# Hybrid conformer and neighbourhood-attention layer: the first two output tiles' preparation, moved behind other work on three queues

## The chip, the cores and the metric

The kernel runs on one core of a Trainium2 chip, in one launch. The metric is the time on the device in microseconds (us). The kernel before took 1469.12 us, the median of 3 runs (1467.73 to 1469.58). TensorE (PE in the rows) multiplies matrices, VectorE (DVE), ScalarE (ACT) and GpSimd (POOL) work on elements, and SyncE (SP) issues all transfers. Each engine runs its own instructions strictly in its queue's order; engines wait for each other by semaphores.

## The reference

One encoder layer over two batches that share all weights: 512 and 1024 tokens, each with 16 meta tokens in front, 1024 channels, float32. In short:

```python
u = rms_norm(h, pre_g)
z = einsum('bld,de->ble', u, w_in)       # 1024 -> 7 x 1024
c_val, c_glu, c_gate, q, k, v, a_gate = split(z)
conv = silu(layer_norm(depthwise_conv31(c_val * sigmoid(c_glu)) + conv_b)) * silu(c_gate)
att  = neighbourhood_attention(q, k, v, meta keys, rel_bias) * silu(a_gate)   # 16 heads of 64
y    = einsum('ble,ed->bld', concat(conv, att), w_out)                        # 2048 -> 1024
out  = h + rms_norm(y, post_g)                                                # meta rows dropped
```

The attention looks at a window of 8 rows by 16 columns of a token grid 64 wide, plus the 16 meta keys, with a relative bias, and takes a softmax over both. The layer norm of the convolution runs over the 1024 channels of a token.

## The kernel before

The 1536 grid tokens are held as three grids of 512 tokens. To keep float32 accuracy each product is three passes of a two-part format (`proj`, L175 to L181: high weights by high input, low weights by high input, high weights by low input). One gate, which is one 128-channel column of one grid, is 24 matmuls of 128x512. ScalarE makes the high part of a weight (L141), GpSimd the low part (L142).

The work goes through these stages:

- The pre-norm, and the input projections.
- The depthwise convolution of 31 taps on VectorE (L272). Its result z goes to memory (`zs`) by channel; the conv gates go to `cgd`.
- The attention in 8 pairs of heads, each with 3 grids and 2 halves (`groups`). For every block of queries: scores on TensorE (L578), reading them with the bias and taking the maximum on VectorE (L585), its negative (L588), the exponential on ScalarE (L589), reciprocal and scaling on VectorE (L590, L591), transposes on TensorE (L600), their copy on ScalarE (L602, `pT`), the weighted product with the values (L616, `po`). At the end of a grid VectorE copies `po` to `mo` (L620), and SP stores it to `mad` (L621). Other projections and gates are put between these steps to fill TensorE.
- The layer norm's statistics are woven into the last pairs (`statistics`, L648 on). Mean and variance of each token go to `std` in memory; at the end the variances come back as `rv`, become 1/sqrt (L678, L679), and are stored again (`std<-rv`, L680), 6 KB in pieces of 4 bytes.
- After the attention, the last six attention gates (`a_gate(6, 7)`): 6 times 24 matmuls, a copy to `ag` on ScalarE (L342), a store to `agd` (L343).
- The output product in 12 tiles of 128 tokens (L794). `load_wo(n)` loads the n-th of 16 row blocks of w_out (L738) into `wraw`, `xr` or `yo`, and makes its high part on ScalarE (L748) and its low part on VectorE (L749).

`mix(t, parts)` (L757 to L774) prepares tile t. Part 0 is the conv half: it loads mean and 1/sqrt (`mb`, L755), z (`mx<-zs`, L764) and the conv gate (`gt<-cgd`, L765), subtracts and multiplies on VectorE (L767, L768), takes 8 silus of 128x128 and one silu of the gate on ScalarE (L770, L771), multiplies them (L772), and makes the high part `mh` on ScalarE (L773) and the low part `ml` on VectorE (L774). Part 1 is the attention half: the same from L771 on, with `mad` and `agd`. TensorE takes the first two tiles together: first half of tile 0, first half of tile 1, second half of tile 0, second half of tile 1, each of 48 matmuls.

What sets the order: the functions are traced in the order in which they are written, and a scheduler with its own model of times then puts each engine's instructions into that engine's queue. `tc.issue_after(ins)` is a tie for it: what is traced under it on the engine of `ins` is queued behind `ins`. It adds no semaphore wait. Tiles 0 and 1 are prepared under such ties: `mix(0, (0,))` behind the last `pT` copy on ScalarE, and `mix(1, (0,))` behind the copy of the last gate, both on ScalarE alone.

Of the kernel before, what the change touches and what calls it, by code (L numbers as in the profile page):

```python
# [13 lines left out]
ALU = mybir.AluOpType  # L14
# [79 lines left out]
def tile_encoder(ctx: ExitStack, tc: tile.TileContext, mt, xn, w_main, w_v, wo, cw, cb, lg, lb, pg, postg, rbt, rmask, y):  # L94
    nc = tc.nc
# [3 lines left out]
    mad = [tc.dram_tile((DC, 128, 512), F32, name=f"mad{g}") for g in range(3)]  # L99
# [46 lines left out]
    def new_mm():  # L146

        pool, tag = banks[1][banks[0] % len(banks[1])]
        banks[0] += 1
        return pool.tile([128, 512], F32, name=tag, tag=tag)  # L150
# [14 lines left out]
    def use_w(ec):  # L165

        w = ahead.pop(ec) if ec in ahead else load_w(ec)
        i = wseq.index(ec) + 1
        if i < len(wseq) and wseq[i] not in ahead:
            ahead[wseq[i]] = load_w(wseq[i])  # L170
        return w
# [3 lines left out]
    def proj(ps, hi, lo, c0, c1):  # L175
        n = c1 - c0
        uh, ul = u_cols(c0, c1)
        for dc in range(DC):
            for i, (w, u) in enumerate(((hi, uh), (lo, uh), (hi, ul))):
                last_mm[0] = nc.tensor.matmul(ps[:, :n], lhsT=w[:, dc, :], rhs=u[dc // 4][:, dc % 4, :],  # L180
                                              start=(dc == 0 and i == 0), stop=(dc == DC - 1 and i == 2)).ins  # L181
# [99 lines left out]
        nc.scalar.copy(out=zc.rearrange("p (b r c) -> p b r c", r=8, c=8), in_=z[:, i].rearrange("p (r b c) -> p b r c", r=8, b=8))  # L281
        nc.sync.dma_start(zs[i][c], zc)

    vws, metas, last_copy = {}, [], [None]

    def load_v(qv):
        raws, his, los = [], [], []
# [46 lines left out]
    def gates(base, dst, cs):  # L334

        ws = [use_w(base + c) for c in cs]
        for g in range(3):
            for c, (wh, wl) in zip(cs, ws):
                ps = new_mm()
                proj(ps, wh, wl, 16 + g * 512, 16 + g * 512 + 512)  # L340
                gt = gpool.tile([128, 512], F32, name="ag", tag="ag", bufs=2)
                last_copy[0] = nc.scalar.copy(out=gt, in_=ps).ins  # L342
                nc.sync.dma_start(dst[g][c], gt)  # L343
                yield

    def c_gate(*cs):
        return gates(16, cgd, cs)

    def a_gate(*ps):
        return gates(40, agd, ps)  # L350
# [192 lines left out]
    def block(g, j):  # L543

        e = ebufs[g][{0: 1, 7: 2}.get(j, 0)]
        if g == 0:
            return min(max(j - 1, 0), 5), 3, "k3", 2, 108, e
        R8 = GR[g]["R"] * 8
        if j in (0, 7):
            return min(j, 6), 2, "k2", 2, R8, e  # L550
        return j - 1, 3, "k3", 3, R8, e

    def load_values(p, g):
        esl = slice(p * 128, p * 128 + 128)
        R8 = GR[g]["R"] * 8
        if g == 0:
            vt = apool.tile([108, 2, 6, 128], F32, name="vp", bufs=VPB)
            for ch, p0, b0, k0, n in ((0, 0, 0, 0, 72), (0, 72, 1, 0, 36), (1, 0, 1, 36, 36), (1, 36, 2, 0, 72)):
                nc.sync.dma_start(vt[p0:p0 + n, ch], vd[b0:b0 + 6, k0:k0 + n, esl].rearrange("b k e -> k b e"))
        else:  # L560
            vt = apool.tile([104, 8, 128], F32, name="vt", bufs=2)
            nc.sync.dma_start(vt[:R8], vd[:, GR[g]["vrow"] * 8:GR[g]["vrow"] * 8 + R8, esl].rearrange("b k e -> k b e"))
        vts[p, g] = vt

    def scores(p, g, hf):
        if hf == 0:
            load_values(p, g)
        kh, kl = kbufs[p]
        qh, ql = qbuf.pop((p, g, hf))
        R8 = GR[g]["R"] * 8  # L570
        for jj in range(4):
            j = hf * 4 + jj
            b0, nk, key, _, _, e = block(g, j)
            ra, rn, ro = GR[g][key]
            w = rn * 8
            ss = ps_s.tile([128, 512], F32, name="ss")
            for i, (q, k) in enumerate(((qh, kh), (qh, kl), (ql, kh))):
                last_qk[0] = nc.tensor.matmul(ss[:, :nk * w], lhsT=q[:, jj].rearrange("p h x -> p (h x)"),  # L578
                                 rhs=k[:, b0:b0 + nk, ra:ra + rn, :].rearrange("p b r c -> p b (r c)"),
                                 start=(i == 0), stop=(i == 2))  # L580
            sv_ = ss[:, :nk * w].rearrange("p (k x) -> p k x", k=nk)[:, :, ro * 8:ro * 8 + R8]
            pt = apool.tile([128, 312], F32, name="pt", bufs=PTB)
            pv = pt[:, :nk * R8]
            sm = apool.tile([128, 4], F32, name="sm", bufs=8)
            nc.vector.tensor_tensor_reduce(out=pv.rearrange("p (k x) -> p k x", k=nk), in0=sv_,  # L585
                                           in1=e.rearrange("p k r c -> p k (r c)"), scale=1.0,
                                           scalar=-3.0e38, op0=ALU.add, op1=ALU.max, accum_out=sm[:, 0:1])
            nc.vector.tensor_scalar(out=sm[:, 1:2], in0=sm[:, 0:1], scalar1=-1.0, scalar2=None, op0=ALU.mult)  # L588
            last[0] = nc.scalar.activation(out=pv, in_=pv, func=AF.Exp, bias=sm[:, 1:2], scale=1.0, accum_out=sm[:, 2:3])  # L589
            nc.vector.reciprocal(sm[:, 3:4], sm[:, 2:3])  # L590
            nc.vector.tensor_scalar(out=pv, in0=pv, scalar1=sm[:, 3:4], scalar2=None, op0=ALU.mult)  # L591
            pts[p, g, j] = pv

    def transposes(p, g, hf):
# [10 lines left out]
    def weighted(p, g, hf):  # L605
        if hf == 0:
            pos[p, g] = ps_o.tile([128, 8, 64], F32, name="po")
        po, vt = pos[p, g], vts[p, g]
        for j in range(hf * 4, hf * 4 + 4):
            b0, _, _, nt, kt, _ = block(g, j)  # L610
            pT = pTs.pop((p, g, j))
            for k in range(nt):
                for h in range(2):
                    hs = slice(h * 64, h * 64 + 64)
                    v = vt[:, k, b0, hs] if g == 0 else vt[:kt, b0 + k, hs]
                    last_pv[0] = nc.tensor.matmul(po[hs, j, :], lhsT=v, rhs=pT[:kt, k * 128 + h * 64:k * 128 + h * 64 + 64],  # L616
                                                  start=(k == 0), stop=(k == nt - 1)).ins
        if hf == 1:
            mo = apool.tile([128, 512], F32, name="mo", bufs=1)
            nc.vector.tensor_copy(out=mo, in_=pos.pop((p, g)).rearrange("p j x -> p (j x)"))  # L620
            nc.sync.dma_start(mad[g][p], mo)  # L621

    def inner_gates():
        for p in (3, 4, 5):
# [56 lines left out]
        yield  # L681

    stats = statistics()
    knext, last_pv, last_pt = [None], [None], [None]
    e_build(0)
    groups = [(p, g, hf) for p in range(NPAIR) for g in range(3) for hf in range(2)]
    for n in range(len(groups) + 2):
        if n < len(groups):
            p, g, hf = groups[n]
# [62 lines left out]
    def moments(t):  # L752
        tsl = slice(t * 128, t * 128 + 128)
        s = std[:, tsl]
        nc.sync.dma_start(mb, bass.AP(s.tensor, s.offset, [[0, 128], [TG, 2], [1, 128]]))  # L755

    def mix(t, parts=(0, 1)):  # L757
        for part in parts:
            if part == 0:
                moments(t)  # L760
            mx, gt = mxs[part], gts[part]
            mh, ml = [x[t % 2 * 2 + part] for x in (mhs, mls)]
            g, csl = t // 4, slice(t % 4 * 128, t % 4 * 128 + 128)
            nc.sync.dma_start(mx, (zs, mad)[part][g][:, :, csl].rearrange("c p t -> p c t"))  # L764
            nc.sync.dma_start(gt, (cgd, agd)[part][g][:, :, csl].rearrange("c p t -> p c t"))  # L765
            if part == 0:
                nc.vector.tensor_tensor(out=mx, in0=mx, in1=mb[:, 0:1].broadcast_to([128, 8, 128]), op=ALU.subtract)  # L767
                nc.vector.tensor_tensor(out=mx, in0=mx, in1=mb[:, 1:2].broadcast_to([128, 8, 128]), op=ALU.mult)  # L768
                for c in range(8):
                    nc.scalar.activation(out=mx[:, c], in_=mx[:, c], func=AF.Silu, scale=lg_sb[:, c:c + 1], bias=lb_sb[:, c:c + 1])  # L770
            nc.scalar.activation(out=gt, in_=gt, func=AF.Silu)  # L771
            nc.vector.tensor_tensor(out=mx, in0=mx, in1=gt, op=ALU.mult)  # L772
            nc.scalar.copy(out=mh, in_=mx)  # L773
            (nc.vector if t < MLT else nc.gpsimd).tensor_tensor(out=ml, in0=mx, in1=mh.bitcast(F32), op=ALU.subtract)  # L774

    with tc.issue_after(last_pt[0]):
        mix(0, (0,))
    for n in range(16):
        if n == 6:
            mix(0, (1,))  # L780
        elif n == 8:
            with tc.issue_after(last_copy[0]):
                mix(1, (0,))
        elif n == 10:
            mix(1, (1,))
        load_wo(n)
    pgb = wop.tile([128, D], F32, name="pgb")
# [28 lines left out]
    for t in range(TG // 128):  # L816
# [26 lines left out]
        for hf in range(2):  # L843
            hsl = slice(hf * 512, hf * 512 + 512)
            nc.vector.scalar_tensor_tensor(out=yo[:, hsl], in0=yo[:, hsl], scalar=s4[:, 3:4], in1=xr[:, hsl],
                                           op0=ALU.mult, op1=ALU.add)
# [65 lines left out]
```

## Time and profile before

| | |
|---|---|
| median of 3 runs | 1469.12 us (1467.73 to 1469.58) |
| the profiled execution | 1470.34 us |
| its span in the trace | 1468.2 us |
| TensorE busy with matmuls | 1437.6 us, 98% of the span |
| VectorE busy | 1012.4 us, 69% |
| ScalarE busy | 562.8 us, 38% |
| GpSimd busy | 254.9 us, 17% |
| TensorE's share of the chain that ended last | 90% |

The profile is of one execution. Busy time tells which engine is full; the view of waits tells what an engine's idle time ended with; the timeline gives single instructions with the idle time in front of them in brackets; the windows give the granted clock of TensorE in a stretch, where 1.00 is 2.4 GHz and 0.50 is 1.2 GHz. The chain of waits is followed back from the last instruction.

### The profile page before, as it was taken

To read this page: it belongs to the slowest core of one execution; us is meant where nothing else is said; L and a number is where in the kernel's file an instruction comes from. 1 tells how busy PE (TensorE), PEld (TensorE's weight loads), DVE (VectorE), ACT (ScalarE), POOL (GpSimd) and SP (SyncE) were. 2 spreads that over 40 slices of the span, in tenths; PEclk is the share of its full clock that TensorE was granted. 3 is DMA by queue.
4 is the path that set the end of the run, shared out by engine and by line. 5 is a ranking of instruction groups with operands and counts; after the bars stand their busy time and mean duration, and the time that the engine had idled before them with its cause. 6 is when DMAs were issued, how large, how long until landed. Compare 5 with 4: busy or idle time off the path is not lost.

```text
span 1468.2 us, 24129 instructions
## 1 busy us (share of the span) xinstructions
PE 1437.6 (98%) x9536; PEld 1239.6 (84%) x9536; DVE 1012.4 (69%) x1739; ACT 562.8 (38%) x1299; POOL 254.9 (17%) x188
## 2 busy tenths in 40 slices
PE   7999999999999999999999999999979989999998
PEld 6988998988998888888888988888868878888886
DVE  6599999998999899846776777767544364342431
ACT  7311112112111111235564555655534466544440
POOL 2042022112101211221111211111101002122120
PEclk9999999999999999999999999999989999999999
DMA  8113113312231212242232232332322495544521
GB/s 266 42 48 117 47 55 110 93 40 93 76 92 50 96 51 86 105 105 75 77 88 79 84 82 77 88 87 83 86 62 87 159 294 145 151 147 136 164 89 43
DMA packets 153464, 145.19 MB, mean 99 GB/s; under 512 B 37216, under 2 KB 125432, under 8 KB 153352
## 3 DMA queue, kind: packets, MB, share of 16 engines
q1 hardware_dynamic: 153352, 143.67, 32.5%
q8 instruction: 74, 1.21, 0.3%
q14 instruction: 38, 0.31, 0.1%
HBM read 105.35 MB, written 42.72 MB: 101 GB/s over the span
## 4 chain that ended last, share of the span: by engine, by line
PE 90%; DMA 4%; ACT 2%; DVE 2%; POOL 1%; issue 1%; DVEq 0%; SPq 0%; ACTq 0%; POOLq 0%
PE mm L180 36%; PE py L794 18%; PE tp L180 9%; PE mm L322 5%; PE ss L578 5%; PE po L180 5%; PE po L616 4%; PE tp L600 4%; PE tp L322 3%; DMA wraw<-in_wo 1%; PE po L322 1%; POOL vl L142 1%; DMA std<-rv 1%; DMA yo<-in_wo 0%; ACT mx L770 0%
## 5 line engine op out<-in xcount | busy, mean ns | idle before, releaser
L180 PE MATMUL mm<-uw,whi 128*128 128x512 f32 (+2 forms) x1904 | 562.1, 372 | 0.0
L272 DVE SCALAR_TENSOR_TENSOR z<-ub,cw_sb,z 128x1536 f32<-128x1536 f32 (+2 forms) x270 | 498.7, 1854 | 8.1
L180 PEld LDWEIGHTS mm<-uw,whi 128*128 128x128 f32 x1904 | 342.5, 188 | 55.4 <-issue 1.3
L180 PE MATMUL mm<-uw,wlo 128*128 128x512 f32 (+2 forms) x952 | 352.6, 371 | 1.1 <-POOL wlo L142 1.1
L142 POOL TENSOR_TENSOR wlo<-wraw,whi 128x1024 fp32r<-128x1024 f32 x48 | 129.0, 2689 | 542.2 <-ACT whi L141 537.5
L180 PEld LDWEIGHTS mm<-uw,wlo 128*128 128x128 f32 x952 | 179.4, 188 | 27.2 <-POOL wlo L142 1.4
L794 PE MATMUL py<-uw,mh 128*128 128x512 f32 x576 | 182.0, 397 | 0.0
L180 PE MATMUL tp<-uw,whi 128*128 128x512 f32 (+2 forms) x512 | 132.9, 344 | 0.0
L589 ACT ACTIVATE pt<-pt,sm 128x216 f32<-128x216 f32 (+4 forms) x192 | 97.2, 507 | 92.9 <-DVE sm L588 79.9
L794 PEld LDWEIGHTS py<-uw,mh 128*128 128x128 f32 x576 | 108.7, 189 | 25.9
L794 PE MATMUL py<-uw,ml 128*128 128x512 f32 x288 | 113.8, 395 | 0.0
L602 ACT COPY pT<-tp 108x256 f32<-108x256 f32 (+4 forms) x192 | 77.9, 419 | 81.9 <-PE tp L600 57.1
L180 PEld LDWEIGHTS tp<-uw,whi 128*128 128x128 f32 x512 | 89.3, 188 | 11.6
L767 DVE TENSOR_TENSOR mx<-mx,mb 128x1024 f32<-128x1024 f32 x12 | 14.7, 1225 | 121.2 <-DMA mx<-zs 110.0
L585 DVE CUSTOM_DVE_ANT_0 pt<-ss,ei 128x216 f32<-128x216 f32 (+2 forms) x144 | 62.6, 437 | 50.2 <-PE ss L578 26.6
L180 PE MATMUL tp<-uw,wlo 128*128 128x512 f32 (+2 forms) x256 | 88.1, 344 | 0.0
L600 PE MATMUL tp<-ident,pt 128*96 128x128 f32 (+2 forms) x480 | 85.5, 275 | 0.3 <-ACT pT L602 0.2
L774 POOL TENSOR_TENSOR ml<-mx,mh 128x1024 fp32r<-128x1024 f32 x20 | 48.2, 2430 | 211.5 <-ACT mh L773 193.7
L322 PE MATMUL mm<-vh,uw 128*128 128x256 f32 x448 | 83.5, 285 | 0.7 <-DVE uw L208 0.5
L591 DVE TENSOR_SCALAR pt<-pt,sm 128x216 f32<-128x216 f32 (+4 forms) x192 | 70.7, 368 | 4.9
L578 PE MATMUL ss<-kh,qh 128*128 128x264 f32 (+3 forms) x192 | 65.3, 340 | 9.0 <-DVE sm L585 9.0
L141 ACT CAST whi<-wraw 128x1024 fp32r<-128x1024 f32 x48 | 50.2, 1047 | 61.6 <-DMA wraw<-in_w_main 19.1
(170 smaller groups left out, 2183.1 us busy)
## 6 DMA issues: line engine op xcount, KB each, us to landing
wraw<-in_w_main SPq DMA_DIRECT2D x48, 512.0 KB
xt<-in_xn SPq DMA_DIRECT2D x12, 512.0 KB
vd<-vs SPq DMA_DIRECT2D x96, 64.0 KB
zs<-zc SPq DMA_DIRECT2D x24, 256.0 KB
cgd<-ag SPq DMA_DIRECT2D x24, 256.0 KB
agd<-ag SPq DMA_DIRECT2D x24, 256.0 KB
ag<-zs SPq DMA_DIRECT2D x24, 256.0 KB
mad<-mo SPq DMA_DIRECT2D x24, 256.0 KB
```

Source lines behind the costliest of these rows:

```text
L142: eng.tensor_tensor(out=lo, in0=raw, in1=hi.bitcast(F32), op=ALU.subtract)
L180: last_mm[0] = nc.tensor.matmul(ps[:, :n], lhsT=w[:, dc, :], rhs=u[dc // 4][:, dc % 4, :], start=(dc == 0 and i == 0), stop=(dc == DC - 1 ...
L272: nc.vector.scalar_tensor_tensor(out=zv, in0=ub[:, a:b, k:k + 512], scalar=cw_sb[:, c, k:k + 1], in1=zv, op0=ALU.mult, op1=ALU.add)
L322: nc.tensor.matmul(ps[:, :256], lhsT=u[dc // 4][:, dc % 4, :], rhs=w[dc // 4][:, dc % 4, :], start=(dc == 0 and i == 0), stop=(dc == DC - ...
L578: last_qk[0] = nc.tensor.matmul(ss[:, :nk * w], lhsT=q[:, jj].rearrange("p h x -> p (h x)"), rhs=k[:, b0:b0 + nk, ra:ra + rn, :].rearrange ...
L585: nc.vector.tensor_tensor_reduce(out=pv.rearrange("p (k x) -> p k x", k=nk), in0=sv_, in1=e.rearrange("p k r c -> p k (r c)"), scale=1.0, ...
L589: last[0] = nc.scalar.activation(out=pv, in_=pv, func=AF.Exp, bias=sm[:, 1:2], scale=1.0, accum_out=sm[:, 2:3])
L591: nc.vector.tensor_scalar(out=pv, in0=pv, scalar1=sm[:, 3:4], scalar2=None, op0=ALU.mult)
L600: nc.tensor.transpose(out=tp[:kt, k * 128:k * 128 + 128], in_=pv[:, k * kt:k * kt + kt], identity=ident)
L602: last_pt[0] = nc.scalar.copy(out=pT[:kt, :nt * 128], in_=tp[:kt, :nt * 128]).ins
L616: last_pv[0] = nc.tensor.matmul(po[hs, j, :], lhsT=v, rhs=pT[:kt, k * 128 + h * 64:k * 128 + h * 64 + 64], start=(k == 0), stop=(k == nt - ...
L794: nc.tensor.matmul(pss[hf], lhsT=m[e // 8][:, e % 8], rhs=w[e][:, hf * 512:hf * 512 + 512], start=(n == 0 and i == 0), stop=(n == 15 and i ...
```

## The change

Three things are moved; no arithmetic is changed, and no instruction of the program's own is added or dropped.

- The first tile's conv half, `mix(0, (0,))`, gets two more ties: on VectorE behind the last scaling of the attention (L591), and on SP behind the next-to-last store of an attention result (L621).
- The second tile's conv half, `mix(1, (0,))`, is tied on ScalarE behind the copy of the fourth of the last six gates in place of the last, and is written at n = 6 of the loop over w_out in place of n = 8.
- The two attention halves are written later: `mix(0, (1,))` at n = 10 in place of 6, and `mix(1, (1,))` at n = 12 in place of 10.

```diff
-    vws, metas, last_copy = {}, [], [None]
+    vws, metas, copies = {}, [], []
...
-                last_copy[0] = nc.scalar.copy(out=gt, in_=ps).ins
+                copies.append(nc.scalar.copy(out=gt, in_=ps).ins)
...
-            nc.vector.tensor_scalar(out=pv, in0=pv, scalar1=sm[:, 3:4], scalar2=None, op0=ALU.mult)
+            last_norm[0] = nc.vector.tensor_scalar(out=pv, in0=pv, scalar1=sm[:, 3:4], scalar2=None, op0=ALU.mult).ins
...
-            nc.sync.dma_start(mad[g][p], mo)
+            stores.append(nc.sync.dma_start(mad[g][p], mo).ins)
...
-    knext, last_pv, last_pt = [None], [None], [None]
+    knext, last_pv, last_pt, last_norm, stores = [None], [None], [None], [None], []
...
-    with tc.issue_after(last_pt[0]):
+    with tc.issue_after(last_pt[0]), tc.issue_after(last_norm[0]), tc.issue_after(stores[-2]):
         mix(0, (0,))
     for n in range(16):
         if n == 6:
-            mix(0, (1,))
-        elif n == 8:
-            with tc.issue_after(last_copy[0]):
+            with tc.issue_after(copies[-3]):
                 mix(1, (0,))
         elif n == 10:
+            mix(0, (1,))
+        elif n == 12:
             mix(1, (1,))
         load_wo(n)
```

The first place is VectorE's queue in the last pair of heads. Here is what stood there before, in the first half of that pair; `mx` and `mb` are the first tile's.

```order
L585 ISA pt,sm<-ss,ei_5362 128x216
L585 ISA sm 128x1
L588 TENSOR_SCALAR sm<-sm 128x1
L590 RECIPROCAL sm<-sm 128x1
L767 TENSOR_TENSOR mx<-mx,mb 128x1024
L591 TENSOR_SCALAR pt<-pt,sm 128x216
L585 ISA pt,sm<-ss,ei_5362 128x216
```

The subtraction L767 stood between two steps of one block's softmax. Now the two steps of the first tile stand after the last block of the attention, between the last two copies of attention results:

```order
L590 RECIPROCAL sm<-sm 128x1
L591 TENSOR_SCALAR pt<-pt,sm 128x208
L620 COPY mo<-po 128x512
L767 TENSOR_TENSOR mx<-mx,mb 128x1024
L768 TENSOR_TENSOR mx<-mx,mb 128x1024
L620 COPY mo<-po 128x512
L772 TENSOR_TENSOR mx<-mx,gt 128x1024
```

The second place is ScalarE's queue during the last gates; `mh_12159` is the result of the second tile's conv half. Before, its 8 silus stood behind the copy of the sixth gate:

```order
L748 CAST uw<-xr 128x1024
L748 CAST uw<-yo 128x1024
L342 COPY ag<-mm 128x512
L770 ACTIVATE mx<-mx,lb_sb,lg_sb 128x128 x8
L771 ACTIVATE gt<-gt 128x1024
L748 CAST uw<-wraw 128x1024
L773 CAST mh_12160<-mx_12153 128x1024
L748 CAST uw<-wraw 128x1024
L773 CAST mh_12159<-mx 128x1024
```

Now they stand behind the fourth gate's copy, which is the first row here, and the fifth gate's copy comes after them:

```order
L342 COPY ag<-mm 128x512
L770 ACTIVATE mx<-mx,lb_sb,lg_sb 128x128 x2
L748 CAST uw<-wraw 128x1024
L770 ACTIVATE mx<-mx,lb_sb,lg_sb 128x128 x6
L771 ACTIVATE gt<-gt 128x1024
L748 CAST uw<-xr 128x1024
L748 CAST uw<-yo 128x1024
L773 CAST mh_12158<-mx_12153 128x1024
L748 CAST uw<-wraw 128x1024
L771 ACTIVATE gt_12154<-gt_12154 128x1024
L342 COPY ag<-mm 128x512
L748 CAST uw<-wraw 128x1024
```

The second tile's `mh_12159` is the row that follows these. The third place is the end of the attention on the same engine. Before, all copies of transposes were done when the gate's copy and the high part of the last gate's weights came:

```order
L602 COPY pT<-tp 104x384 x3
L602 COPY pT<-tp 104x256
L770 ACT_TABLE_LOAD
L770 ACTIVATE mx<-mx,lb_sb,lg_sb 128x128 x8
L771 ACTIVATE gt<-gt 128x1024
L342 COPY ag<-mm 128x512
L141 CAST whi<-wraw 128x1024
```

Now both stand in front of the last of these copies:

```order
L602 COPY pT<-tp 104x384 x4
L342 COPY ag<-mm 128x512
L141 CAST whi<-wraw 128x1024
L602 COPY pT<-tp 104x256
L770 ACT_TABLE_LOAD
L770 ACTIVATE mx<-mx,lb_sb,lg_sb 128x128 x8
```

The order of the attention's own steps in the last pair is also reshuffled by the scheduler, on TensorE, VectorE and ScalarE alike.

## Rows read from the trace of the kernel before

**Rows 1.** Page part 1: busy time, share of the span, instructions.

```profile
PE 1437.6 (98%) x9536; PEld 1239.6 (84%) x9536; DVE 1012.4 (69%) x1739; ACT 562.8 (38%) x1299; POOL 254.9 (17%) x188
```

**Rows 2.** Waits of TensorE: us in total, times, longest.

```profile
PE ss L578 <- DVE sm L585: 9.0, 2, 8.7
PE ss L202 <- DVE un L196: 8.4, 1, 8.4
PE py L794 <- ACT mh L773: 3.9, 1, 3.9
```

**Rows 3.** Timeline of TensorE: start, us, operation, count, idle time before and its end.

```profile
1079.24 0.59 PE L578 MATMUL ss<-kh,qh 128*128 128x264 f32 x1 [8.74 <-DVE sm L585]
...
1203.37 0.79 PE L794 MATMUL py<-woh,mh 128*128 128x512 f32 x1 [3.92 <-ACT mh L773]
```

**Rows 4.** Timeline of VectorE around the first wait.

```profile
1077.42 1.22 DVE L767 TENSOR_TENSOR mx<-mx,mb 128x1024 f32<-128x1024 f32 x1 [11.22 <-DMA mb<-std]
1078.56 0.33 DVE L591 TENSOR_SCALAR pt<-pt,sm 128x216 f32<-128x216 f32 x1
1078.81 0.38 DVE L585 CUSTOM_DVE_ANT_0 pt<-ss,ei 128x216 f32<-128x216 f32 x1
```

**Rows 5.** Chain that ended last: start, us, what.

```profile
1062.39 10.93 DMA std<-rv
1073.34 4.05 DMA mb<-std
...
1080.27 2.56 PE mm L180 x6
...
1083.37 2.53 PE mm L180 x11
...
1187.44 6.44 DMA yo<-in_wo
```

**Rows 6.** Windows: us, PE, PEld, DVE, ACT, POOL busy, PEclk, DMA share, GB/s.

```profile
112.00:114.00 2.00, 0.92 (x5) 0.53 (x3) 2.00 (x1) 1.31 (x3) 1.97 (x1) 1.00 0.41 96
...
1079.20:1083.10 3.90, 3.86 (x12) 3.15 (x13) 2.98 (x9) 2.02 (x6) 0.00 (x0) 0.50 0.13 34
...
1203.40:1209.40 6.00, 6.00 (x14) 4.74 (x15) 5.44 (x5) 3.72 (x4) 0.00 (x0) 0.50 1.02 274
1209.40:1215.00 5.60, 5.60 (x25) 4.49 (x25) 2.45 (x2) 2.28 (x6) 0.00 (x0) 1.00 0.51 159
```

**Rows 7.** Timeline of ScalarE, from the attention's end to the second tile.

```profile
1151.04 0.75 ACT L602 COPY pT<-tp 104x384 f32<-104x384 f32 x2 [4.19 <-PE tp L600]
...
1153.10 3.19 ACT L770 ACTIVATE mx<-mx,lb_sb,lg_sb 128x128 f32<-128x128 f32 x8
...
1157.61 1.05 ACT L141 CAST whi<-wraw 128x1024 fp32r<-128x1024 f32 x1
...
1194.92 0.58 ACT L342 COPY ag<-mm 128x512 f32<-128x512 f32 x1
1195.40 3.20 ACT L770 ACTIVATE mx<-mx,lb_sb,lg_sb 128x128 f32<-128x128 f32 x8
...
1202.27 1.05 ACT L773 CAST mh<-mx 128x1024 fp32r<-128x1024 f32 x1
```

**Rows 8.** Timeline of VectorE at the end of the attention.

```profile
1153.80 0.69 DVE L620 COPY mo<-po 128x512 f32<-128x512 f32 x1 [14.41 <-PE po L616]
```

**Rows 9.** Timeline of TensorE: last weighted product, and an earlier short wait.

```profile
114.03 0.39 PE L180 MATMUL mm<-uw,wlo 128*128 128x272 f32 x1 [1.11 <-POOL wlo L142]
...
1152.25 1.50 PE L616 MATMUL po<-pT,vt 104*64 104x64 f32 x44
```

**Rows 10.** Page part 5: costliest groups, count, busy us, mean ns, idle before.

```profile
L589 ACT ACTIVATE pt<-pt,sm 128x216 f32<-128x216 f32 (+4 forms) x192 | 97.2, 507 | 92.9 <-DVE sm L588 79.9
L585 DVE CUSTOM_DVE_ANT_0 pt<-ss,ei 128x216 f32<-128x216 f32 (+2 forms) x144 | 62.6, 437 | 50.2 <-PE ss L578 26.6
L591 DVE TENSOR_SCALAR pt<-pt,sm 128x216 f32<-128x216 f32 (+4 forms) x192 | 70.7, 368 | 4.9
```

## The prediction, made before the changed kernel had run

> **What bounds the kernel.** I read the busy times first. TensorE works in 98% of the span [rows 1], so a change of order can only win where TensorE stands still or runs slowly. The view of its waits comes next [rows 2]: three waits are over 3 us, one at the start of the kernel (8.4 us, on the pre-norm, which the change doesn't touch), one of 8.7 us on a VectorE step of the attention (L585), one of 3.9 us on ScalarE's `mh` (L773). The last two are in the stretches that the change touches. The timeline gives their places: TensorE stood for 8.74 us until 1079.24, and for 3.92 us until 1203.37 [rows 3].
>
> Who made the first one? VectorE's timeline shows L767, which belongs to the first output tile, in front of a scaling and a score reading of the attention [rows 4]. It stood for 11.22 us until `mb` had landed, and only behind it came L585, for which TensorE waited. The chain tells why `mb` was late: the store of the statistics began at 1062.39 and took 10.93 us, though the table of 1/sqrt is small, and the load behind it took 4.05 us [rows 5]. So a tile whose product starts only some 100 us later held up the attention.
>
> The second: the last gate's copy ran at 1194.92, the 8 silus behind it from 1195.40 to 1198.6, and `mh` from 1202.27 [rows 7]. The copy was itself late because the weight conversions in front of it in ScalarE's queue waited for a load that started at 1187.44 and took 6.44 us [rows 5]. TensorE had used up what it could do at 1203.37 − 3.92 = 1199.45.
>
> Both waits leave a second loss, seen in the windows: behind each the granted clock is 0.50, that is 1.2 GHz in place of 2.4 GHz, for 3.90 us after the first and 6.00 us after the second, and then 1.00 again [rows 6].
>
> **What the change removes.**
>
> 1. First wait: 8.74 us. Half clock behind it: 6 matmuls of L180 took 2.56 us there, 0.427 each, and 11 of them a little later 2.53 us, 0.230 each [rows 5]. So 3.90 us of that work would have taken 3.90 × 0.230/0.427 = 2.1, a loss of 1.8. Together 10.5.
> 2. Second wait: 3.92 us. Behind it 14 matmuls took 6.00 us [rows 6]; at 0.23 each, 3.2. Loss 2.8. Together 6.7.
>
> The sum of both is 17.2 us, if nothing takes their place.
>
> **What comes at the first tile's new place.** The two VectorE steps now stand between the last two copies L620. VectorE was idle there for 14.41 us until 1153.80, so from 1139.4 on [rows 8]. SP issues the tile's loads behind the store that follows the copy before that gap, so at about 1140. If `mb` takes 4.05 us and a 512 KB load 6.44 (the slowest such row I use) one behind the other [rows 5], the data are there at 1150.5, and two steps of 1.22 us [rows 4] end at 1152.9. The silus began at 1153.10 before [rows 7], behind the last transposes' copies, and are queued there still. So at the slowest in series the steps just end in time, and with the loads side by side some 4 us early; and this tile isn't wanted until the six gates are done, 144 × 0.230 = 33 us after the last weighted product. I cost it at nothing; the idle VectorE and the gates hide it. If that cover were gone the last copy L620 would wait, which holds nothing for TensorE but the attention half of the tiles, later still. SP has one thing less to wait for: the load of `mb` no longer stands in its queue behind the slow store of 10.93 us, so gate stores and weight loads queued behind it go out earlier, and I count nothing for this.
>
> **What comes at the second tile's new place.** I keep the old clock of the trace to see who is late. The last weighted product ended at 1152.25 + 1.50 = 1153.75 [rows 9]. With the cost of the next paragraph 1154.45. The fourth gate is done 96 × 0.230 = 22.1 us later, at 1176.5, and its copy (0.58 us, [rows 7]) at 1177.1. Behind it ScalarE does, up to the second tile's `mh`: 8 silus, 3.20 us; nine instructions of 1.05 us (conversions of weights, silus of gates, two `mh`), 9.45; and the fifth gate's copy, 0.58 [rows 7]. Together 13.2, so 1190.3. The weight loads in between could hold it: the queues carry loads of 6.44 us at worst [rows 5], and following the buffers with that landing for each load gives 1191.3. TensorE gets to the second tile after 144 + 48 matmuls: 1154.45 + 192 × 0.230 = 1198.6. The margin is 7 to 8 us, so the second wait goes wholly. What is late next are the attention halves, written 4 and 2 steps later now. They are wanted 48 and 96 matmuls later (11 and 22 us); ScalarE has for each only a silu, a conversion and its neighbours, so I find over 10 us of margin there. The fifth and sixth gates' copies now stand behind the silus: about 13 us at most, in a stage in which TensorE has other banks for its products and the output matmuls to go on with. Cost nothing.
>
> **What the change adds.** At the end of the attention the gate's copy and the conversion `whi` stand now in front of the last copy of transposes on ScalarE. The last weighted products wait for that copy, and TensorE with them. The trace of before has no such wait. At the one end, nothing: the gate's end and the weights may be early enough. At the other, copy and conversion run wholly in front, 0.58 + 1.05 = 1.63 us [rows 7]. A gain from it is excluded, since nothing on TensorE's path moves ahead. I take 0.7, below the middle, because ScalarE was idle 4.19 us just before that copy [rows 7] and part of the work falls into such a gap.
>
> The reshuffle of the attention's steps: the same instructions, with TensorE and VectorE in another order. Before, outside the stall, TensorE waited for L585 only 9.0 − 8.7 = 0.3 us in the whole kernel [rows 2]. I take nothing here as well; the bounds are in the rivals.
>
> **Sum.** 17.2 − 0.7 = 16.5 us of the profiled execution's 1470.34 us. That is 1.2 us above the median of the runs, so on the median: 1469.1 − 16.5 = 1452.6, which I round to 1452.5.
>
> **Rivals.**
>
> - *The second wait stays.* The silus move, but the `mh` behind them hangs on loads that hang on buffers that hang on VectorE's low parts; if one of those links is 8 us later than I followed it, ScalarE stands again, as it did for the load at 1187.44. For it: DMA share is 1.02 around 1203 to 1209 [rows 6], so loads are slow there. Against: the margin of 7 to 8 us already has 6.44 us for every load. Then only the first part is won: 1469.1 − 10.5 + 0.7 = 1459.3.
> - *The first wait only moves:* another step of the first tile or the store behind it gets in the attention's way, and only the second is won: 1469.1 − 6.7 + 0.7 = 1463.1. Against: the tie puts both steps behind the last L591, as the order shows, so this is the case in which the change doesn't do what it says.
> - *The new short wait costs the clock too.* What the rows show is a wait of 1.11 us at 114.03 [rows 9] in a window with the clock at 1.00 [rows 6], so a wait of that length left the clock whole; by that 0.7 us costs 0.7. Against me would be a half-clock stretch behind it as behind the two waits, 1.8 to 2.8 us: 1455. The Trainium skill, "TensorE: Matmul & The Clock Gate", section "A second HAM failure mode: psum-queue depth-cycling", speaks for this: it says that small idle gaps between groups of matmuls can be enough to make the clock fall and rise, with a cost each time. By that rule the time would be this rival's 1455; the trace, so far, agrees with the row at 114.03 instead.
> - *The reshuffled attention becomes a chain.* By the order of the queues 22 scores lie between the old place of the first wait and the end of the attention. If the new order makes TensorE wait, block by block, for reading, exponential and scaling of the block before, each costs up to 0.437 + 0.507 + 0.368 = 1.31 us [rows 10], 22 × 1.31 = 28.9 us, and the time is 1452.5 + 28.9 = 1481.4: slower than before. It decides from 16.5/22 = 0.75 us a block on; with reading and scaling alone (0.81) it would be 1470.2. For it: hundreds of places in TensorE's order differ. Against: VectorE had slack there, up to 14.41 us at a time near the end [rows 8], and the softmax of one block usually lies beside the projections that fill the gap.
>
> **Chances.** Forecast 0.72; second wait stays 0.09; clock lost too 0.06; first wait only moved 0.04; attention a chain 0.09. The last splits by its price per block: 0.01 still faster, 0.03 within 0.2%, 0.05 slower. 0.2% is 2.9 us, about what a measurement of this kernel can tell from no change. Faster: 0.72 + 0.09 + 0.06 + 0.04 + 0.01 = 0.92. Same 0.03, slower 0.05.
>
> The range: at the low end the added wait is nothing (1451.9) and some 2 us are left for the spread of the runs and for SP's earlier loads: 1450. At the high end the range takes in the full 1.63 us of the added wait (1453.5), the clock rival and the case in which the second wait stays (1459.3): 1459.5. That leaves out the moved wait and the chain, 0.13.
>
> **What would show it.** In the waits of TensorE of the changed kernel, the 8.7 us on L585 and the 3.9 us on L773 should be gone, and the windows should have no stretch at 0.50 near the first half of the last pair nor at the second tile. A wait of 0 to 1.6 us of L616 for the last `pT` should appear, at clock 1.00 behind it. L767 should wait for nothing that is followed by an attention step. It would be wrong if L773 is still in the list with over 2 us, if L578 or L600 collect several us of short waits in the last pair, or if the clock falls behind the new wait.

## The result, and the profile after

The changed kernel took 1453.35 us, the median of 4 runs (1452.55 to 1453.64), against 1469.06 us before. The ratio is 0.9894, with a 95% interval of 0.9876 to 0.9911. That is 15.7 us less. The forecast was 1452.5 us.

The profiled execution took 1453.64 us with a span of 1451.4 us. Page part 1 of the changed kernel, in the columns of [rows 1]:

```profile
PE 1434.7 (99%) x9536; PEld 1238.8 (85%) x9536; DVE 1012.5 (70%) x1739; ACT 563.5 (39%) x1299; POOL 255.8 (18%) x188
```

The waits of TensorE, which answer to [rows 2]:

```profile
PE ss L202 <- DVE un L196: 8.2, 1, 8.2
PE mm L180 <- POOL wlo L142: 1.1, 1, 1.1
PE po L616 <- ACT pT L602: 0.5, 1, 0.5
...
PE tp L600 <- ACT pT L602: 0.2, 1, 0.2
```

Both waits are gone, the 8.7 us on L585 and the 3.9 us on L773. One short wait is new, that of the last weighted products L616 for the copy of transposes. Its place on TensorE's timeline, with the moment at which the second tile's first matmul ran:

```profile
1143.48 0.45 PE L616 MATMUL po<-pT,vt 104*64 104x64 f32 x8 [0.48 <-ACT pT L602]
...
1188.01 0.40 PE L794 MATMUL py<-woh,mh 128*128 128x512 f32 x1
```

The window around that short wait, in the columns of [rows 6], has the clock at 1.00:

```profile
1143.00:1145.00 2.00, 1.52 (x14) 1.27 (x14) 0.69 (x1) 1.97 (x4) 1.77 (x1) 1.00 0.54 171
```

VectorE's timeline at the first tile's new place answers to [rows 8]:

```profile
1129.35 0.68 DVE L620 COPY mo<-po 128x512 f32<-128x512 f32 x1
1138.91 1.23 DVE L767 TENSOR_TENSOR mx<-mx,mb 128x1024 f32<-128x1024 f32 x1 [8.88 <-DMA mx<-zs]
1140.17 1.22 DVE L768 TENSOR_TENSOR mx<-mx,mb 128x1024 f32<-128x1024 f32 x1
1143.98 0.69 DVE L620 COPY mo<-po 128x512 f32<-128x512 f32 x1 [2.58 <-PE po L616]
```

L767 still waits 8.88 us for a load, but nothing is queued behind it that TensorE needs: the next copy L620 came when its product was done, and 2.58 us were left.

ScalarE's timeline, in the form of [rows 7], at the end of the attention and at the second tile:

```profile
1141.62 0.59 ACT L342 COPY ag<-mm 128x512 f32<-128x512 f32 x1 [2.46 <-PE mm L180]
1142.11 1.05 ACT L141 CAST whi<-wraw 128x1024 fp32r<-128x1024 f32 x1
1143.05 0.38 ACT L602 COPY pT<-tp 104x256 f32<-104x256 f32 x1
...
1169.02 0.57 ACT L342 COPY ag<-mm 128x512 f32<-128x512 f32 x1
1169.49 0.88 ACT L770 ACTIVATE mx<-mx,lb_sb,lg_sb 128x128 f32<-128x128 f32 x2
...
1180.64 1.04 ACT L773 CAST mh<-mx 128x1024 fp32r<-128x1024 f32 x1
```

The second tile's `mh` was ready at 1181.7, and TensorE wanted it at 1188.0: a margin of 6.3 us, where the prediction had 7 to 8.

### The profile page after: what moved, and what is told of

The parts are those of the page before. It is cut to its first block, busy times and chain, and to the rows that moved or that the text cites. A ratio compares the mean times of both kernels' runs of the same rounds, so it can differ in the third digit from the quotient of the medians.

```text
span 1451.4 us, 24134 instructions
## 1 busy us (share of the span) xinstructions
PE 1434.7 (99%) x9536; PEld 1238.8 (85%) x9536; DVE 1012.5 (70%) x1739; ACT 563.5 (39%) x1299; POOL 255.8 (18%) x188
## 4 chain that ended last, share of the span: by engine, by line
PE 96%; POOL 1%; DVE 1%; DMA 1%; ACT 1%; issue 0%; DVEq 0%; SPq 0%; ACTq 0%; POOLq 0%
PE mm L180 39%; PE py L794 18%; PE tp L180 9%; PE mm L322 6%; PE ss L578 5%; PE po L180 5%; PE po L616 4%; PE tp L600 4%; PE tp L322 3%; POOL vl L142 1%; PE po L322 1%; PE ss L202 0%; DMA gb<-in_pg 0%; PE tp L202 0%; PE mm L664 0%; DMA wraw<-in_w_main 0%
## 5 line engine op out<-in xcount | busy, mean ns | idle before, releaser
L794 PE MATMUL py<-uw,mh 128*128 128x512 f32 x576 | 180.9, 395 | 0.0
L794 PEld LDWEIGHTS py<-uw,mh 128*128 128x128 f32 x576 | 108.1, 188 | 25.4
L794 PE MATMUL py<-uw,ml 128*128 128x512 f32 x288 | 113.3, 394 | 0.0
L767 DVE TENSOR_TENSOR mx<-mx,mb 128x1024 f32<-128x1024 f32 x12 | 16.1, 1340 | 120.8 <-DMA mx<-zs 120.8
L585 DVE CUSTOM_DVE_ANT_0 pt<-ss,ei 128x216 f32<-128x216 f32 (+2 forms) x144 | 62.6, 437 | 45.4 <-PE ss L578 22.9
L774 POOL TENSOR_TENSOR ml<-mx,mh 128x1024 fp32r<-128x1024 f32 x20 | 48.5, 2441 | 216.4 <-ACT mh L773 216.4
L591 DVE TENSOR_SCALAR pt<-pt,sm 128x216 f32<-128x216 f32 (+4 forms) x192 | 71.7, 373 | 4.9
L141 ACT CAST whi<-wraw 128x1024 fp32r<-128x1024 f32 x48 | 50.3, 1047 | 61.1 <-DMA wraw<-in_w_main 18.6
L180 PE MATMUL po<-uw,whi 128*128 128x512 f32 (+2 forms) x272 | 72.9, 347 | 0.0
```

The lines of the kernel that those rows point to most:

```text
L591: last_norm[0] = nc.vector.tensor_scalar(out=pv, in0=pv, scalar1=sm[:, 3:4], scalar2=None, op0=ALU.mult).ins
L794: nc.tensor.matmul(pss[hf], lhsT=m[e // 8][:, e % 8], rhs=w[e][:, hf * 512:hf * 512 + 512], start=(n == 0 and i == 0), stop=(n == 15 and i ...
```

## The experiments

All times are medians of runs in which kernel and kernel before took turns on one chip; the medians of the kernel before lay between 1468.15 and 1469.20 us. In some of these kernels the line numbers are shifted by up to 8 lines; the text names the line of the kernel before where it matters.

**Each part alone.** The first kernel has the changed ties of the first tile and the old loop. Against the changed kernel:

```diff
         if n == 6:
-            with tc.issue_after(copies[-3]):
-                mix(1, (0,))
-        elif n == 10:
             mix(0, (1,))
-        elif n == 12:
+        elif n == 8:
+            with tc.issue_after(copies[-1]):
+                mix(1, (0,))
+        elif n == 10:
             mix(1, (1,))
```

> Only the first tile's two new ties; the second tile stays behind the sixth gate's copy and the halves are written where they were. My theory (two separate waits, each a matter of one place in a queue): the 8.7 us wait on L585 and its half-clock stretch are gone, the 3.9 us wait on L773 stays with its half clock. From the changed kernel's 1453.4 plus 6.7: about 1460, 8 to 10 us under the kernel before. Rival (the second wait was a result of the first one's delay, and goes with it): 1453 to 1455. Rival (the first tie alone only pushes the wait elsewhere): 1466 or more.

Measured: 1453.21 us, ratio 0.9895 [0.9882, 0.9909]. My expectation of 1460 failed. The first part alone gives the whole gain. Its waits of TensorE:

```profile
...
PE po L616 <- ACT pT L602: 0.5, 1, 0.5
PE mm L322 <- DVE uw L208: 0.4, 1, 0.4
PE py L794 <- ACT mh L773: 0.3, 1, 0.3
```

The second wait is down to 0.3 us though the 8 silus stand behind the sixth gate's copy, as before. The second kernel has the loop of the change and the first tile's old tie:

```diff
-    with tc.issue_after(last_pt[0]), tc.issue_after(last_norm[0]), tc.issue_after(stores[-2]):
+    with tc.issue_after(last_pt[0]):
         mix(0, (0,))
```

> Only the second part: the second tile behind the fourth gate's copy, written at n = 6, and the halves at 10 and 12; the first tile has its old tie alone. My theory: TensorE still waits 8.7 us for L585 with the half clock behind it, nothing at L773, and no wait for the last transposes' copy, since that copy stands in front of the weight conversion again. 1453.4 + 10.5 - 0.5 = 1463. Rival (the first tile's lateness decides the second tile too): the wait on L773 is still over 2 us and the time 1466 to 1469.

Measured: 1464.76 us, ratio 0.9969 [0.9958, 0.998], so 4.1 us under the kernel before. Its waits of TensorE:

```profile
PE ss L578 <- DVE sm L585: 9.5, 1, 9.5
PE ss L202 <- DVE un L196: 8.2, 1, 8.2
...
```

L794 isn't in the list. The first wait stays (0.75 us longer here), and the second is gone. So each part alone removes the second wait; 15.6 of the one and 4.1 of the other are not to be added. The second part by itself works as I had said. What I had not seen is that the first part does it too.

**The tie without the new places.** Here the second tile is tied behind the fourth gate, with everything written at the old n; against the first kernel above:

```diff
         elif n == 8:
-            with tc.issue_after(copies[-1]):
+            with tc.issue_after(copies[-3]):
                 mix(1, (0,))
```

> The changed kernel with the attention halves written where they were before (n = 6 and 10) and the second tile's conv half at n = 8, but tied behind the fourth gate's copy. My theory (the place of the 8 silus on ScalarE decides): they start early, the high part stands some instructions later than in the changed kernel; the wait on L773 is 0 to 1.5 us, the time 1453 to 1456. Rival (the writing places decide, since they set the order of the loads): the wait stays 3 to 4 us with its half clock, 1459 to 1461.

Measured: 1454.00 us, ratio 0.99 [0.9886, 0.9913], no wait on L773. That agrees with my expectation, but after the first kernel it decides nothing, since the first tile's ties, which this one has too, suffice.

**Whether SP's standing costs anything.** The change without the tie on SP:

```diff
-    with tc.issue_after(last_pt[0]), tc.issue_after(last_norm[0]), tc.issue_after(stores[-2]):
+    with tc.issue_after(last_pt[0]), tc.issue_after(last_norm[0]):
         mix(0, (0,))
```

> The changed kernel without the tie on SP: VectorE's two steps stay behind the attention, but the load of the means stands on SP right behind the slow store of the statistics again, with gate stores and a weight load behind it. My theory (VectorE's queue alone made the first wait): SP stands for about 11 us and TensorE does not notice; 1453 within 1.5, no wait on L578. Rival (SP's standing delays gate stores or weights that TensorE needs): a wait of 3 us or more in the last pair, 1456 to 1464.

Measured: 1453.18 us, ratio 0.9895 [0.988, 0.991]. SP's timeline shows the load of the means waiting for the slow store:

```profile
1062.35 0.36 SPq L680 DMA_DIRECT2D std<-rv  x1
1073.86 0.36 SPq L755 DMA_DIRECT2D mb<-std  x1
1074.31 0.42 SPq L343 DMA_DIRECT2D agd<-ag  x1
```

Between these two, from 1062.35 to 1073.86, SP issued nothing, and TensorE had no wait there. So the slow store did harm only through VectorE's queue. The other way round, with the tie on SP and without that on VectorE, the scheduler gives every engine the same order as in the changed kernel. So the tie on VectorE adds nothing to the one on SP, and either does. That the reshuffled order of the attention's steps has no part in it is argued, not shown: it came with the ties, and no run has it alone. For the queue alone speaks that L767 and its 11.22 us stood directly in front of the scaling and the L585 for which TensorE waited [rows 4].

**Why the first part removes the second wait.** The new theory starts from ScalarE and SP. In the kernel before, the conversion `whi` of the last gate's weights stood behind the first tile's 8 silus, at 1157.61 [rows 7]. The weights' buffer, `wraw`, is one of two that the w_out blocks use as well, so the second w_out load could go only after it and after the low part that GpSimd makes from the same buffer. SP's timeline of the kernel before has that load:

```profile
1162.27 0.33 SPq L738 DMA_DIRECT2D wraw<-in_wo  x1
```

ScalarE's timeline of the same kernel has its conversion, which waited for it:

```profile
1168.10 1.05 ACT L748 CAST woh<-wraw 128x1024 fp32r<-128x1024 f32 x1 [7.06 <-DMA wraw<-in_wo]
```

With the first tile's ties `whi` comes before the last copy of transposes. In the kernel with the first part alone SP's timeline has the load here:

```profile
1144.78 0.83 SPq L738 DMA_DIRECT2D wraw<-in_wo  x1
```

And ScalarE's timeline there, at the attention's end and at the sixth gate's copy:

```profile
1141.24 1.05 ACT L141 CAST whi<-wraw 128x1024 fp32r<-128x1024 f32 x1
1142.19 0.38 ACT L602 COPY pT<-tp 104x256 f32<-104x256 f32 x1
...
1179.80 1.05 ACT L748 CAST uw<-yo 128x1024 fp32r<-128x1024 f32 x1 [0.60 <-DMA yo<-in_wo]
1180.76 0.58 ACT L342 COPY ag<-mm 128x512 f32<-128x512 f32 x1
1181.23 3.19 ACT L770 ACTIVATE mx<-mx,lb_sb,lg_sb 128x128 f32<-128x128 f32 x8
```

TensorE's timeline there has the end of the weighted products:

```profile
1142.62 0.45 PE L616 MATMUL po<-pT,vt 104*64 104x64 f32 x8 [0.48 <-ACT pT L602]
```

Counted from that end (1153.75 before, 1142.62 + 0.45 = 1143.07 here), that load went out after 8.5 us before and after 1.7 us now, and the sixth gate's copy ran after 41.2 us before and 37.7 us now. The chain that ended last, in this kernel's profile, runs from `whi` over GpSimd's low part and the loads to that copy:

```profile
1142.37 2.39 POOL wlo L142
1144.76 0.02 issue
1144.78 4.29 DMA wraw<-in_wo
...
1173.74 5.99 DMA yo<-in_wo
```

So the theory is that the move which I priced as the cost of the change starts the chain of w_out loads earlier, and that this chain held the sixth gate's copy. Three runs test that.

The first has this move alone, in the kernel before (`last_cast` is the instruction of L141):

```diff
-    with tc.issue_after(last_pt[0]):
+    with tc.issue_after(last_cast[0]):
         mix(0, (0,))
```

> The kernel before with one thing changed: the first tile's conv half is tied on ScalarE behind the conversion of the last gate's weights in place of the last transposes' copy, so that this conversion stands in front of the 8 silus. New theory (the second wait came from the chain of w_out loads, which starts when the gate's weight buffer is free, and that conversion frees it): the first wait stays, 8.7 us; the first loads of w_out go out some 5 us earlier, the sixth gate's copy is no longer held, and the wait on L773 is 0 to 1 us: 1463 to 1465, as where only the second part was made. My old theory (the place of the second tile's silus behind the sixth gate decides): that place is as before, so the wait stays 3 to 4 us, 1468 to 1469.

Measured: 1464.90 us, ratio 0.998 [0.997, 0.9991], with a wide spread of 1462.84 to 1468.59. Its waits of TensorE (L796 is the kernel before's L794):

```profile
PE ss L580 <- DVE sm L587: 8.4, 1, 8.4
PE ss L204 <- DVE un L198: 8.1, 1, 8.1
...
PE py L796 <- ACT mh L775: 0.9, 1, 0.9
```

Its second load of w_out and its sixth gate's copy, from SP's and ScalarE's timelines:

```profile
1155.23 0.33 SPq L740 DMA_DIRECT2D wraw<-in_wo  x1
```

```profile
1190.90 0.57 ACT L344 COPY ag<-mm 128x512 f32<-128x512 f32 x1
```

The weighted products ended at 1152.58 here, so the load went out after 2.7 us and the copy ran after 38.3. The first wait stays and the second falls to 0.9 us, as the new theory says. That is the profiled execution (1463.37 us). Of nine executions five took 1462.84 to 1464.90 us, and four 1466.51 to 1468.59, about as long as the kernel before beside it (1466.94 to 1469.90). Their mean granted clocks, 0.994 to 0.995 against 0.995 to 0.996 of the five, are about those of the kernel before too. That fits a second wait which came back in these four with its half clock, but no trace shows one of them. So this move alone is worth the second wait in some executions only, while the whole first part was worth it in all four of its own (1452.57 to 1454.07).

The second run undoes the early load in the kernel with the first part alone:

```diff
-        nc.sync.dma_start(raw, wo[e])
+        if n == 1:
+            with tc.issue_after(gstores[-6]):
+                nc.sync.dma_start(raw, wo[e])
+        else:
+            nc.sync.dma_start(raw, wo[e])
```

`gstores` lists the stores of the gates, L343.

> The kernel with the first tile's ties alone (1453.2), and the load of the second row block of w_out tied on SP behind the first store of the last six gates, which is about where it went out in the kernel before (8.5 us after the last weighted product in place of 1.7). New theory: the load chain is late again, the sixth gate's copy is held by conversions, and the wait on L773 comes back with 3 to 5 us and half clock behind it: 1458 to 1461. Rival (the second wait went because the first tile's loads and silus moved): it stays away, 1453 to 1454.

Measured: 1457.13 us, ratio 0.9919 [0.9905, 0.9932], 3.9 us above the kernel without that edit. The wait is back. TensorE's wait on L798, its timeline behind the wait, the window there, and ScalarE (here L774 to L777 are L770 to L773, L798 is L794):

```profile
PE py L798 <- ACT mh L777: 3.3, 1, 3.3
```

```profile
1194.36 0.50 PE L798 MATMUL py<-woh,mh 128*128 128x512 f32 x1 [3.33 <-ACT mh L777]
```

```profile
1194.30:1200.00 5.70, 5.64 (x24) 4.56 (x25) 4.59 (x4) 3.97 (x5) 0.00 (x0) 1.00 0.85 264
```

```profile
1182.12 1.05 ACT L752 CAST uw<-wraw 128x1024 fp32r<-128x1024 f32 x1 [3.69 <-DMA wraw<-in_wo]
1183.08 1.04 ACT L777 CAST mh<-mx 128x1024 fp32r<-128x1024 f32 x1
1184.03 1.05 ACT L752 CAST uw<-xr 128x1024 fp32r<-128x1024 f32 x1
1184.98 0.57 ACT L342 COPY ag<-mm 128x512 f32<-128x512 f32 x1
```

A conversion that waited 3.69 us for its load stands in front of the sixth gate's copy, as one that waited 1.83 us did in the kernel before. The time is 0.9 us below the range that I expected, since no half clock followed. The third run puts the same late load into the whole change:

> The whole change with the same late load. New theory: the second part of the change is a second cure for the same wait, so with the silus behind the fourth gate the late chain is borne: the wait on L773 is 0 to 1 us, 1453 to 1455. Rival (the second part does nothing on the chip): 1458 to 1461, as with the first ties alone and the late load.

Measured: 1452.83 us, ratio 0.9893 [0.988, 0.9907], no wait on L794. So the second part bears the late chain which the first part alone does not. It is a second cure for the same wait.

**Is it the late load, or what stands in front of the copy?** Two runs. One makes the load later still, with `gstores[-5]` in place of `gstores[-6]`:

> The first tile's ties alone, with the load of the second row block tied behind the second store of the last six gates, about 4 us later than in the run that brought the wait back. If the load chain sets the wait, it grows from 3.3 us to 5 to 7 us, and if a wait longer than the 3.9 us of the kernel before brings the half clock with it, another 2 to 3 us go: 1460 to 1465. If the chain is not what sets it, the wait stays at 3 us and the time at 1457. If the clock stays whole behind a wait of 5 to 7 us: 1459 to 1461.

Measured: 1453.05 us, ratio 0.9895 [0.988, 0.9909], and no wait. My expectation failed. ScalarE's timeline tells why:

```profile
1179.02 1.05 ACT L752 CAST uw<-wraw 128x1024 fp32r<-128x1024 f32 x1
1180.21 1.06 ACT L775 ACTIVATE gt<-gt 128x1024 f32<-128x1024 f32 x1
1181.17 0.57 ACT L342 COPY ag<-mm 128x512 f32<-128x512 f32 x1
1181.64 3.19 ACT L774 ACTIVATE mx<-mx,lb_sb,lg_sb 128x128 f32<-128x128 f32 x8
```

The scheduler put the conversions of the tenth to twelfth blocks behind the silus, I take it because it models the load as later. So the copy ran at 1181.17 in place of 1184.98. The last run makes only this move, in the kernel whose wait had come back (there the tenth and the eleventh stood in front of the copy):

```diff
-        nc.scalar.copy(out=h, in_=raw)
+        if n in (9, 10, 11):
+            with tc.issue_after(copies[-1]):
+                nc.scalar.copy(out=h, in_=raw)
+        else:
+            nc.scalar.copy(out=h, in_=raw)
```

> The run that brought the wait back (first ties alone, second row block loaded late, 1457.1), with one edit more: the conversions of the tenth to twelfth row blocks are tied on ScalarE behind the sixth gate's copy. Their loads go out in the same order. If the wait came from late loads held in front of that copy, the silus start some 3 us earlier and the wait of 3.3 us shrinks to 0 to 1.5 us: 1453 to 1455.5. If the loads' lateness alone sets it, wherever the conversions stand, it stays 3 us: 1457.

Measured: 1453.43 us, ratio 0.9896 [0.9879, 0.9912]. The wait fell from 3.3 to 1.0 us, and the copy ran earlier, as TensorE's waits and ScalarE's timeline show:

```profile
PE py L802 <- ACT mh L781: 1.0, 1, 1.0
```

```profile
1182.18 0.58 ACT L342 COPY ag<-mm 128x512 f32<-128x512 f32 x1
```

So it takes both: loads that are late, and their conversions in front of the sixth gate's copy. Take away either and the wait goes, or nearly. The six kernels in which the silus stand behind that copy agree on it, each by its own profile:

| kernel | end of the weighted products | sixth gate's copy | from the one to the other | wait for `mh` |
|---|---|---|---|---|
| before | 1153.75 | 1194.92 | 41.2 us | 3.9 us |
| first part, late load | 1144.23 | 1184.98 | 40.8 | 3.3 |
| the same, conversions behind the copy | 1143.81 | 1182.18 | 38.4 | 1.0 |
| before, `whi` first | 1152.58 | 1190.90 | 38.3 | 0.9 |
| first part | 1143.07 | 1180.76 | 37.7 | 0.3 |
| first part, load later still | 1143.99 | 1181.17 | 37.2 | none |

In each of the first five the wait is the time in the fourth column less 37.2 to 37.5 us, and in the sixth, where the copy comes by then, there is none. So in these kernels the moment of the sixth gate's copy sets the wait.

**A better version?** The whole change with `whi` tied behind the last copy of transposes should save the new wait of 0.5 us:

```diff
-        nc.scalar.copy(out=hi, in_=raw)
+        with tc.issue_after(last_pt[0]) if last_pt[0] is not None and len(stores) == 24 else nullcontext():
+            nc.scalar.copy(out=hi, in_=raw)
```

> The whole change with the conversion of the last gate's weights tied behind the last transposes' copy, to save the new wait of 0.5 us on L616. The gate's copy still stands in front, so the wait should shrink to about 0.1 us and the time by 0.3 to 0.4 us: 1453.0, not to be told from the changed kernel. If the later conversion made the load chain late it would be 1454 or more.

Measured: 1452.45 us, ratio 0.989 [0.9877, 0.9904]. It was repeated beside the changed kernel:

> The changed kernel again, for the comparison with the next one on the same chip: 1453 within 1.

> The whole change with the conversion of the last gate's weights behind the last transposes' copy, beside the changed kernel on the same chip. The trace of its first run has no wait on L616, so 0.5 us less than the changed kernel if nothing else moves; a difference under 1 us is not to be told from none.

Measured: 1452.76 us (1452.51 to 1453.07) for the changed kernel and 1452.84 us (1452.02 to 1454.23) for this one. The wait on L616 is gone from its trace, but the time can't be told from the changed kernel's.

## Why the prediction was right, and where its working was not

- **First wait.** Right in mechanism, and about right in size. I had 10.5 us. The kernel that keeps this wait is 1464.76 − 1453.35 = 11.4 us above the changed one, which has the new wait of 0.48 us in its place; so the first wait was worth 11.9 us there. It was 9.49 us long in place of 8.74, which accounts for 0.75 of the 1.4 us between.
- **Second wait.** Right that it goes, and right that the place of the silus would do it alone (1464.76 us, no wait on L794). What was wrong is the step that followed the load chain only as a risk for the rival "the second wait stays". I had named the late load as the reason for the late copy, but not seen that the change brings the load forward: in "What the change adds" I priced the earlier `whi` only as a cost and wrote "A gain from it is excluded, since nothing on TensorE's path moves ahead", and of SP's earlier loads I wrote that I count nothing for them. The runs show the gain: the first part alone brings the wait down to 0.3 us, and the load made late again brings it back to 3.3. The forecast of the sum stood because either part removes the same wait; the gain does not split as I had split it, and my expectation for the first part alone, 1460 us, was 6.8 us off.
- **Size of the second wait.** I had 6.7 us from the profiled execution. Over the medians it is worth less, if the first is worth 10.5: 15.7 + 0.5 for the new wait − 10.5 = 5.7 us by the whole change, and 4.1 + 0.75 = 4.9 by the second part alone. The profiled execution of the kernel before was 1.3 us above its median, which is about as much: between the profiled executions, 1470.34 and 1453.64, the difference is 16.7 us against the 16.5 forecast. I took a sum made for this slower execution off the median; that explains most of the 0.85 us between forecast and result. Which of the two waits is longer in a slower execution no trace shows.
- **The new wait.** 0.48 us, within the bounds of 0 to 1.63, with the clock whole behind it. The rival "the clock too" fell.
- **The first tile at its new place.** Right: loads issued at 1130.4 and after, two steps ended at 1141.4, and the silus began at 1144.7; 8.88 us of waiting on VectorE cost TensorE nothing.
- **The reshuffled attention.** No wait on L578 is left at all, so the rival on the slower side had no price.
- **The rule on the clock.** The row at 114.03 had been the better guide: behind 0.48 us, and in one experiment behind 3.33 us, the granted clock stayed at 1.00. The Trainium skill, "TensorE: Matmul & The Clock Gate", section "A second HAM failure mode: psum-queue depth-cycling", describes small gaps that come often between groups of matmuls and cost the clock; behind these single short gaps it did not fall, so no run here shows that. A clock of 0.50 stood behind the waits of 3.92 and 8.74 us of the kernel before [rows 6].

## What to carry to other kernels

A wait in an in-order queue can come from something two queues away, as the second one here: look which buffer the late load waits for, and what stands in front of the instruction that frees it. When a change has two parts, run each alone before crediting a gain to it; here the first part carried the second gain too, by way of the move that I had priced as a cost, and the part meant for it was a spare. An instruction with a slow input is harmless where nothing that the bounding engine needs is queued behind it.

## What the runs showed of the hardware that I had not expected

I had taken for granted that a wait of TensorE such as the second one costs its clock. Not each does. After the wait of 3.92 us in the kernel before it stood at 0.50 for 6.00 us [rows 6]; after a wait of 3.33 us at the same place in the program it stood at 1.00 for the next 5.70 us. So of two waits 0.6 us apart in length one cost 2.8 us more than itself and the other about nothing. These are one profile each; what decides between them the runs don't show.
